# Gate's early load behind a piece of w_in, a fourth place in the rings of the output columns, and a seventh pair of seven products

## The chip, the cores and the metric

The kernel runs on one core of one Trainium2 chip. The metric is the device time of one execution in microseconds (us), lower is better. The kernel before has a median of 918.88 us in three runs (916.53 to 919.73).

Engines are called by their names in the profile: PE multiplies matrices (PEld loads its stationary operand), DVE and ACT work elementwise, POOL too, SP issues most of the DMA transfers. Each engine, and SP's queue of transfers too, works strictly in the order in which its instructions stand; an instruction that has to wait holds up all behind it.

## The reference

One layer of a decoder on 256 tokens (T), width D = 2048, inner width E = 4096, all in float32:

```python
h = rmsnorm(x, norm_g)                                  # (1, 256, 2048)
mod = einsum('bd,df->bf', silu(c), ada_w) + ada_b       # ada_w: 2048 x 6144
shift, scale, gate = split(mod, 3)
h = h * (1 + scale) + shift
proj = einsum('bsd,de->bse', h, w_in)                   # w_in: 2048 x 16384
b_gate, c_gate, v, g = split(proj, 4)
u = causal_depthwise_conv(c_gate * v, conv_w)           # width 3
y = b_gate * u * silu(g)                                # (1, 256, 4096)
out = rmsnorm(x + gate * einsum('bse,ed->bsd', y, w_out), final_g)   # w_out: 4096 x 2048
```

Of the 218 MB of weights most is w_in (134 MB); every weight is read once or, with the sums below, a little more.

## The kernel before

**High and low parts.** PE works on a rounded float32 here. Each float32 operand is split into a high part (a cast on ACT, L380) and a low part (what is left, a subtraction on DVE, L385), and each product is the sum of three: high by high, high by low, low by high. So a piece of weights that comes in as `raw` needs a place for its high part `hi` and one for its low part `lo`. The transposed activations `hT` hold both parts already: k 0 to 13 (blocks of 128 of D) in one tile `big`, k 14 and 15 in `big2`.

**Rings.** A place holds 2048 float32 columns on 128 partitions (1 MB). `w_tile(kind, ...)` hands out places in rings of three: "raw", "hi" and "lo". In the second phase "raw" takes the pieces of w_in and "lo" their low parts. In the output phase it is the other way round: the pieces of w_out and the sums made of them lie in the ring "lo", their low parts in the ring "raw"; only pair 0 of the first columns is loaded into the ring "raw".

**First phase** (up to 377 us): the first half of w_in, and the sums of silu(c) with ada_w for shift and scale. Nothing of it changes.

**Second phase** (loop at L798): the channel tiles 16 to 31 in twos, four quarters of w_in each (b_gate, c_gate, v, g), two pieces of eight k each: 64 pieces of 1 MB, loaded by SP (L804). A piece costs PE 48 matmuls of 128x256 into the bank `mm_b` (L545). At the end of a quarter DVE and ACT take the bank away (L827, L828, L830). Behind each piece stand two calls:

- `gate_piece()`: one of 32 pieces of the gate's sums over ada_w (loads `at_g`, sums on DVE in `gacc`, L711). When a quarter of the gate is complete, POOL folds its 128 partitions in seven steps, a DMA and an addition each (L715 to L717), and adds the row to `gate_row` in DRAM.
- `early_weights()`: a table `EARLY`, by the count of pieces, says what else is done. For a pair of `SEVEN_2` it loads a block of w_out (`raw_u`, L755), makes its sums on DVE (L769, L772, L773) and stores them to DRAM from ACT's queue (`made`, L780). "gate" loads a quarter of `gate_row` into `turned` (L786), which is the tile z0 and so in the trace `z<-gate_row`; POOL's folds use the same tile `turned`. "gated" multiplies a block of w_out with it.

**Output** (`columns`, L943): y by w_out. A pair is 256 of the 4096 channels. The first call makes the output's first 1024 columns from all 16 pairs (`mm_w`, matmuls 128x512, L888), the second the next 512 columns and, for the pairs it has, the last 512 (`mm_o`). A plain pair costs 24 matmuls. A pair in `SEVEN` or `SEVEN_2` costs 21: instead of the eight products of 2 x 2 blocks by 2 x 2 blocks it makes seven (`seven`, L904), from sums of the weights' blocks (`sums_o`, made by DVE at L769 to L773, or loaded from `made`) and from sums of the tokens (`form`). In the banks `mm_1` and `mm_7` the products stand that `gather` adds afterwards. Then come pairs 4 to 7 for the third 512 columns, the gated blocks for the last 512, and the residual, norm and stores.

In the first columns pieces and sums go round in six places (`wide_ring`): the three of the ring "lo" and three in the tile `big`, in which hT lay. From n = 13 (`AT_END`) on, `big` takes half of x, final_g and u2. In the second columns they go round in four (`next_ring`) until twelve are given out, then in three.

**What sets the order.** The code's order is only a start: a scheduler puts each engine's instructions in order by when it expects places and operands to come free. Starts that are pinned by `add_manual_dep` come behind the instruction they name.

Of the kernel before, what the change touches and what calls it, by code (L numbers as in the profile page):

```python
# [13 lines left out]
P = 128  # L14
# [103 lines left out]
def short_conv_layer(ctx: ExitStack, tc: tile.TileContext, x, c, norm_g, ada_w, ada_b, w_in, conv_w, w_out, final_g, out):  # L118
# [21 lines left out]
    nth = {"raw": 0, "hi": 0, "lo": 0}  # L140

# [157 lines left out]
    junk = hpool.tile([P, TT, HX], F32, tag="big", name="junk")  # L299
# [18 lines left out]
    KB = KT - 2  # L318
    hT = hpool.tile([P, KB, 2 * T], F32R, tag="big", name="hT")
    hT2 = hpool.tile([P, KT - KB, 2 * T], F32R, tag="big2", name="hT2")  # L320

    def tokens(k, part):
        return (hT[:, k] if k < KB else hT2[:, k - KB])[:, part * T : (part + 1) * T]
# [352 lines left out]
    def gate_columns(c0, n):  # L676
        flat = gate_slots[c0 // 1024].rearrange("p h s f -> p (h s f)").bitcast(F32)
        return flat[:, c0 % 1024 : c0 % 1024 + n]
# [3 lines left out]

    def load_gate(j):

        c0 = j * 1024
        nc.sync.dma_start(gate_columns(c0, 1024), gate_row[0:1, c0 : c0 + 1024].partition_broadcast(P))
# [38 lines left out]
    SEVEN_2 = range(10, 16)  # L725
# [39 lines left out]
    passed = [0]  # L765

# [8 lines left out]
    def early_weights():  # L775

        while to_store:
            unit, sums = to_store.pop()
            made[unit] = dram.tile([P, SLOT], F32, tag=f"made{len(made)}", name="made")
            nc.scalar.dma_start(made[unit], sums)  # L780
        unit = EARLY.get(passed[0])
        passed[0] += 1
        if unit is None:
            return
        if unit == "gate":
            nc.sync.dma_start(turned, gate_row[0:1, 3 * W : 4 * W].partition_broadcast(P))  # L786
            return
        raw, sums = raw_tile("raw_u"), w_tile("lo", "sums_u")
        blocks, out = (v.rearrange("p (b f) -> p b f", f=W) for v in (raw, sums))
        if not isinstance(unit, int):  # L790
            load_o(raw, unit[1] * EP, EP, 3 * W, W)
            nc.vector.tensor_tensor(out=out, in0=blocks, in1=turned.unsqueeze(1).to_broadcast([P, EP, W]), op=ALU.mult)
        else:
            load_o(raw, 2 * unit, 2, 2 * W, 2 * W)
            list(sums_of(blocks, out))
        to_store.append((unit, sums))

    for ct in range(NS, NCT, 2):  # L798
        for q in QUARTERS:
            bank = psum.tile([P, CT, T], F32, tag="mm", name="mm_b")[:, 0:2]  # L800
            col = q * E + ct * P
            for kp in range(0, KT, KP):
                raw = raw_tile("raw")
                nc.sync.dma_start(  # L804
# [34 lines left out]
    big = hpool.tile([P, 3 * D + W], F32, tag="big", name="big")  # L839
    xh = big[:, 0 : TT * D].rearrange("p (h t f) -> p h t f", h=2, t=TT)  # L840
    HD = D // 2

    def xr(t, c0, n):
        return xh[:, c0 // HD, t, c0 % HD : c0 % HD + n]

    def load_x(h):
        for t in range(TT):
            nc.sync.dma_start(xh[:, h, t], x[t * P : (t + 1) * P, h * HD : (h + 1) * HD])

    fg = big[:, TT * D : 3 * D]  # L850
    u2 = big[:, 3 * D :]
    ends = [z.rearrange("p a b f -> p (a b f)").rearrange("p (h f) -> p h f", h=2) for z in zs]

    places6 = [None] * 3 + [big[:, i * SLOT : (i + 1) * SLOT] for i in range(3)]
    taken, ending = [0], [False]

    def wide_ring(name):

        i = taken[0] % 6 if not ending[0] else 0
        taken[0] += 1  # L860
        return w_tile("lo", name) if places6[i] is None else places6[i]
# [12 lines left out]
    last_silu = ended_silu[0]  # L874
# [22 lines left out]
    def weighted(t, c0, n, pr, at):  # L897
# [4 lines left out]
        nc.vector.tensor_tensor(out=r, in0=r, in1=fg[:, c0 : c0 + n], op=ALU.mult)  # L902
# [40 lines left out]
    def columns(c0, order, sevens, bank, p1, p6, p75, whole, loads=None, ring=None):  # L943


        for n, j in enumerate(order):
            raw = w_tile("raw", "raw_o") if n == 0 and c0 == 0 else ring("raw_o")
# [10 lines left out]
            if j in sevens:  # L958
                sums = ring("sums_o")
# [20 lines left out]
    def wide_bank(name):  # L980
# [6 lines left out]
        lambda t, d: wide[t][:, d], *extra_banks(), p75, True, load_ends, wide_ring,  # L987
# [10 lines left out]
    def finish(t):  # L998
# [4 lines left out]
        for c0, n, vector in ((0, 512, True), (512, 512, False), (1536, 512, True), (1024, 512, False)):  # L1003
            dd = slice(c0, c0 + n)
            r = xr(t, c0, n)
            if c0 == 1536:
                nc.vector.scalar_tensor_tensor(out=r, in0=po[t], scalar=fs, in1=fg[:, dd], op0=ALU.mult, op1=ALU.mult)
# [5 lines left out]

    AT_X = 8
    taken[0] = 0

    def next_ring(name):

        i = taken[0] % 4
        taken[0] += 1  # L1020
        return big[:, SLOT : 2 * SLOT] if i == 3 and taken[0] <= 12 else w_tile("lo", name)

# [4 lines left out]
        2 * W, (0, 1, 10, 2, 11, 3, 12, 13, 8, 14, 15, 9), SEVEN_2,  # L1027
        lambda t, d: halves[d][:, t], *po, p75, False, lambda n: load_x(1) if n == AT_X else None, next_ring,
# [81 lines left out]
```

## Time and profile before

| | us |
|---|---|
| median of 3 runs | 918.88 |
| the profiled execution, its time | 917.02 |
| its span | 915.2 |
| PE busy | 888.6 |
| DVE busy | 695.4 |
| ACT busy | 490.5 |
| POOL busy | 88.0 |

The profile is of one execution. The span is what lies between its first and last instruction; 1.8 us of the execution's time lie around it. The mean granted clock of PE is 0.991. In the rows that are shown below, a timeline has the start, the duration, the engine with its line, the operation, what it writes and reads, the shape and the count, and in brackets the idle time before it with what ended that. A row of the windows has the stretch and its length, then busy time and count of PE, PEld, DVE, ACT and POOL, PE's granted clock, the DMA engines' busy share and GB/s. A row of the DMA issues has the count, KB each and the median time from issue to landing. A row of the waits has the sum, the count and the longest.

### The profile page before, as it was taken

The page shows a single profiled execution, that of the slowest core. Times are in us where ns is not written, and L with a number is a line of the kernel's source. Part 1 is how long each engine was busy: PE and PEld are TensorE (multiplying, and loading weights), DVE is VectorE, ACT ScalarE, POOL GpSimd, SP SyncE. Part 2 cuts the span into 40 slices and gives each one's busy share as a digit, 9 for nine tenths or more (in the row PEclk, how much of TensorE's full clock was granted, in tenths as well). Part 3 has the DMA queues.
Part 4 walks back from the last instruction along what each step waited for, and adds up shares of the span by engine and source line. Part 5 has one row for each costly group of instructions (what it writes and reads, how often), then busy time and mean ns, then how long its engine had stood idle before and what let it go on. Part 6 is the DMA issues. An engine that isn't in the chain of part 4 may idle for free.

```text
span 915.2 us, 16520 instructions
## 1 busy us (share of the span) xinstructions
PE 888.6 (97%) x6977; PEld 849.9 (93%) x6977; DVE 695.4 (76%) x693; ACT 490.5 (54%) x436; POOL 88.0 (10%) x108
## 2 busy tenths in 40 slices
PE   7999999999999999999999999949999999999996
PEld 4999999999999999999999999949999988778885
DVE  5889998889987876858865786537667668999775
ACT  6768866565558765644344434234434454545553
POOL 0000000010000234410132012400000000000000
PEclk9999999999999999999999999979999999999999
DMA  9999999999997688777877889489889877686872
GB/s 307 368 370 365 365 321 354 341 363 351 380 344 258 189 279 238 237 215 222 271 230 219 273 270 307 142 286 301 290 286 289 306 264 244 197 294 235 302 280 92
DMA packets 164873, 257.29 MB, mean 281 GB/s; under 512 B 7668, under 2 KB 106580, under 8 KB 162624
## 3 DMA queue, kind: packets, MB, share of 16 engines
q1 hardware_dynamic: 159680, 239.89, 79.5%
q0 software_dynamic: 3840, 7.94, 3.2%
q10 hardware_dynamic: 1280, 8.43, 2.3%
q8 instruction: 54, 0.88, 0.4%
q14 instruction: 19, 0.16, 0.0%
HBM read 237.86 MB, written 10.50 MB: 271 GB/s over the span
## 4 chain that ended last, share of the span: by engine, by line
PE 79%; DMA 11%; DVE 4%; ACT 2%; POOL 2%; issue 1%; SPq 0%; ACTq 0%; POOLq 0%; DVEq 0%
PE mm_s L545 38%; PE mm_b L545 27%; PE mm_o L888 6%; PE mm L888 4%; DMA z<-gacc 3%; PE mm_w L888 3%; DMA at_g<-in_ada_w_dram 3%; DVE lo L385 2%; DMA at<-in_ada_w_dram 2%; ACT hi L380 2%; POOL gacc L717 1%; DMA raw_o<-in_sc_w_out_dram 1%; DMA raw<-in_sc_w_in_dram 1%; POOL z L715 0%; DVE gacc L711 0%
## 5 line engine op out<-in xcount | busy, mean ns | idle before, releaser
L545 PE MATMUL mm_b<-hT,hi 128*128 128x256 f32 x2048 | 349.9, 277 | 11.4 <-ACT hi L380 11.4
L545 PE MATMUL mm_s<-hT,hi 128*128 128x256 f32 x2048 | 336.3, 277 | 0.0
L545 PEld LDWEIGHTS mm_b<-hT,hi 128*128 128x128 f32 x2048 | 309.3, 188 | 11.6 <-ACT hi L380 11.6
L545 PEld LDWEIGHTS mm_s<-hT,hi 128*128 128x128 f32 x2048 | 299.7, 188 | 0.2
L545 PE MATMUL mm_b<-hT,lo 128*128 128x256 f32 x1024 | 283.4, 277 | 1.5 <-DVE lo L385 1.5
L545 PE MATMUL mm_s<-hT,lo 128*128 128x256 f32 x1024 | 261.7, 277 | 0.0
L380 ACT CAST hi<-raw 128x2048 fp32r<-128x2048 f32 (+1 forms) x66 | 123.8, 1876 | 206.9 <-PE mm_b L545 94.0
L385 DVE TENSOR_TENSOR lo<-raw,hi 128x2048 fp32r<-128x2048 f32 (+1 forms) x66 | 153.3, 2328 | 78.6 <-ACT hi L380 63.1
L545 PEld LDWEIGHTS mm_b<-hT,lo 128*128 128x128 f32 x1024 | 192.9, 188 | 1.8 <-DVE lo L385 1.8
L545 PEld LDWEIGHTS mm_s<-hT,lo 128*128 128x128 f32 x1024 | 182.7, 188 | 0.0
L385 DVE TENSOR_TENSOR lo<-raw_s,hi 128x2048 fp32r<-128x2048 f32 (+1 forms) x80 | 149.0, 1868 | 29.9 <-ACT hi L380 29.3
L380 ACT CAST hi<-raw_s 128x2048 fp32r<-128x2048 f32 (+2 forms) x81 | 124.0, 1541 | 70.2 <-PE mm_s L545 42.9
L515 DVE SCALAR_TENSOR_TENSOR gv<-at,silu_c,gv 128x512 f32<-128x512 f32 x105 | 78.8, 751 | 10.3 <-DMA at<-in_ada_w_dram 8.6
L568 ACT COPY acc<-mm_s 128x1024 f32<-128x1024 f32 x54 | 54.6, 1011 | 26.9 <-PE mm_s L545 26.8
L717 POOL TENSOR_TENSOR gacc<-gacc,z 128x512 f32<-128x512 f32 x28 | 44.2, 1577 | 103.4 <-DMA z<-gacc 103.4
L888 PE MATMUL mm_w<-hi,y 128*128 128x512 f32 x160 | 51.4, 390 | 0.3 <-ACT hi L380 0.3
L711 DVE SCALAR_TENSOR_TENSOR gacc<-at_g,silu_c,gacc 128x512 f32<-128x512 f32 x60 | 45.0, 749 | 7.4 <-DMA at_g<-in_ada_w_dram 6.3
L888 PE MATMUL mm_o<-hi,y 128*128 128x512 f32 x152 | 48.3, 389 | 0.0
L582 ACT COPY mm_s<-acc 128x1024 f32<-128x1024 f32 x38 | 38.6, 1015 | 2.6 <-DVE acc L571 1.8
L380 ACT CAST hi<-raw_o 128x2048 fp32r<-128x2048 f32 x14 | 26.7, 1909 | 22.1 <-DMA raw_o<-in_sc_w_out_dram 16.8
L385 DVE TENSOR_TENSOR lo<-raw_o,hi 128x2048 fp32r<-128x2048 f32 x14 | 32.1, 2289 | 6.8 <-ACT hi L380 6.7
L888 PEld LDWEIGHTS mm_w<-hi,y 128*128 128x128 f32 x160 | 30.0, 188 | 6.9 <-ACT hi L380 0.7
(191 smaller groups left out, 745.6 us busy)
## 6 DMA issues: line engine op xcount, KB each, us to landing
raw<-in_sc_w_in_dram SPq DMA_DIRECT2D x64, 1024.0 KB, 6.2
raw_s<-in_sc_w_in_dram SPq DMA_DIRECT2D x47, 1024.0 KB, 8.2
at<-in_ada_w_dram SPq DMA_DIRECT2D x126, 256.0 KB, 7.9
raw_o<-in_sc_w_out_dram SPq DMA_DIRECT2D x17, 1024.0 KB, 6.0
raw_s<-in_sc_w_in_dram SPq DMA_DIRECT2D x33, 512.0 KB, 7.2
at_g<-in_ada_w_dram SPq DMA_DIRECT2D x32, 512.0 KB, 8.2
raw_u<-in_sc_w_out_dram SPq DMA_DIRECT2D x8, 1024.0 KB, 5.7
made<-sums_u ACTq DMA_DIRECT2D x8, 1024.0 KB, 6.9
```

The lines of the kernel that those rows point to most:

```text
L380: nc.scalar.copy(hi[:, :n], raw[:, :n])
L385: last_low[0] = nc.vector.tensor_tensor(out=lo[:, :n], in0=raw[:, :n], in1=hi[:, :n].bitcast(F32), op=ALU.subtract)
L515: nc.vector.scalar_tensor_tensor(out=gv, in0=at4[:, i], scalar=c_k, in1=gv, op0=ALU.mult, op1=ALU.add)
L545: mm = last_mm[0] = nc.tensor.matmul(dst, w, h[k], start=begins and left, stop=ends, skip_group_check=True)
L568: nc.scalar.copy(acc[ch, q], bank)
L582: nc.scalar.copy(bank, acc[ch, q])
L711: nc.vector.scalar_tensor_tensor(out=ga, in0=at3[:, i, :], scalar=s, in1=ga, op0=ALU.mult, op1=ALU.add)
L717: nc.gpsimd.tensor_tensor(out=ga, in0=ga, in1=turned, op=ALU.add)
L888: nc.tensor.matmul(dst, y[a], b, start=opens and i == 0, stop=ends and i == 2, skip_group_check=True)
```

## The change

1. hT lies in five tiles: `b0`, `b1`, `b2` (k 0 to 3, 4 to 7, 8 to 11; a place each), `b3` (k 12, 13) and `big2` (k 14, 15). So a part of it comes free when the last matmul on these k is done.
2. From the start of the output, `fourth` gives each of the rings "lo", "hi" and "raw" a fourth place: b0, b1, b2. This holds for the first columns until n = 10. From n = 13 on b0 takes half of x, b2 (`closing`) half of final_g and half of the gate, and b1 is the fourth place of "lo", until n = 5 of the second columns. `places6`, `wide_ring` and `next_ring` are gone.
3. `SEVEN_2` has a seventh pair, 9, and the second columns another order. Its early units stand at every third count from 33 instead of every fourth from 35, and the other three units at 56, 58, 61 instead of 58, 59, 62.
4. The early load of the gate is tied behind the load of the piece of w_in that was issued last in the code.

```diff
     def w_tile(kind, name, dtype=F32, i=None):
         if i is None:
-            i = nth[kind] % 3
-            nth[kind] += 1
+            size = 4 if kind in fourth else 3
+            i = nth[kind] % size
+            nth[kind] = i + 1
+        if i == 3:
+            return hpool.tile([P, SLOT + 64], dtype, tag=fourth[kind], name=name)[:, 16 : 16 + SLOT]
         return wpool.tile([P, SLOT], dtype, tag=f"{kind}{i}", name=name, bufs=1)
...
-    KB = KT - 2
-    hT = hpool.tile([P, KB, 2 * T], F32R, tag="big", name="hT")
-    hT2 = hpool.tile([P, KT - KB, 2 * T], F32R, tag="big2", name="hT2")
+    hT = [hpool.tile([P, SLOT + 64], F32R, tag=f"b{g}", name="hT") for g in range(3)]
+    hT += [hpool.tile([P, 4 * T], F32R, tag=tag, name="hT") for tag in ("b3", "big2")]
...
-    SEVEN_2 = range(10, 16)
+    SEVEN_2 = range(9, 16)
...
-    EARLY = {35 + 4 * i: j for i, j in enumerate(SEVEN_2)}
-    EARLY.update({58: "gate", 59: ("gated", LAST[0]), 62: ("gated", LAST[1])})
+    EARLY = {33 + 3 * i: j for i, j in enumerate(SEVEN_2)}
+    EARLY.update({56: "gate", 58: ("gated", LAST[0]), 61: ("gated", LAST[1])})
...
         if unit == "gate":
-            nc.sync.dma_start(turned, gate_row[0:1, 3 * W : 4 * W].partition_broadcast(P))
+            load = nc.sync.dma_start(turned, gate_row[0:1, 3 * W : 4 * W].partition_broadcast(P))
+            tc.add_manual_dep(load.ins, last_load[0].ins.name, after, reason="the gate is done by then")
             return
...
-                nc.sync.dma_start(
+                last_load[0] = nc.sync.dma_start(
...
     def load_ends(n):
-        ending[0] = n >= AT_END
-        if n == AT_END - 2:
-            load_gate(0)
+        if n == AT_END - 3:
+            fourth.clear()
         elif n == AT_END:
             load_x(0)
-        elif n == AT_END + 1:
-            nc.sync.dma_start(fg, final_g.rearrange("(o d) -> o d", o=1).partition_broadcast(P))
-            load_gate(1)
+            closing.append(hpool.tile([P, D], F32, tag="b2", name="closing"))
+            load_fg(0)
+            load_broadcast(HD, gate_row[0:1, 0:HD])
+            fourth["lo"] = "b1"
+    fourth.update({"lo": "b0", "hi": "b1", "raw": "b2"})
...
-            raw = w_tile("raw", "raw_o") if n == 0 and c0 == 0 else ring("raw_o")
+            raw = w_tile("raw" if n == 0 and c0 == 0 else "lo", "raw_o")
...
+    def load_last(n):
+        if n == AT_X - 3:
+            fourth.clear()
+        elif n == AT_X:
+            load_x(1)
+            nc.sync.dma_start(gate_columns(HD, HD), gate_row[0:1, HD:D].partition_broadcast(P))
+            load_fg(1)
...
-        2 * W, (0, 1, 10, 2, 11, 3, 12, 13, 8, 14, 15, 9), SEVEN_2,
+        2 * W, (0, 9, 1, 10, 11, 2, 12, 13, 3, 14, 15, 8), SEVEN_2,
```

SP's queue in the second phase, before, around the gate load (`z0`): raw are pieces of w_in, raw_u the blocks of the early units.

```order
L755 DMA raw_u_6749<-in_sc_w_out_dram 128x2x1024 [waits DMAHW7_49,DMAHW4_49,DVE_49]
L804 DMA raw_6763<-in_sc_w_in_dram 128x8x256 [waits DMAHW5_49,DVE_49]
L804 DMA raw_6819<-in_sc_w_in_dram 128x8x256 [waits DMAHW6_49,DMAHW1_49,DVE_49]
L804 DMA raw_6876<-in_sc_w_in_dram 128x8x256 [waits DMAHW7_49,DVE_49]
L804 DMA raw_6930<-in_sc_w_in_dram 128x8x256 [waits DMAHW0_49,DVE_49]
L755 DMA raw_u_6984<-in_sc_w_out_dram 128x2x1024 [waits DMAHW1_49,DVE_49]
L786 DMA z0_4482<-gate_row_4486 128x512 [waits DMASW4_49,DMASW3_49,DMASW5_49,DMASW2_49,DMASW6_49,DMASW1_49,DMASW7_49,DMASW0_49,Pool_49]
L804 DMA raw_7001<-in_sc_w_in_dram 128x8x256 [waits DMAHW3_49,DVE_49]
L804 DMA raw_7057<-in_sc_w_in_dram 128x8x256 [waits DMAHW4_49,DVE_49]
```

The same queue after, around the same load, now L789; the first raw_u shown is that of the seventh pair, and the line numbers of the others are L757 for L755 and L808 for L804.

```order
L757 DMA raw_u_7712<-in_sc_w_out_dram 128x2x1024 [waits DMAHW7_49,DVE_49]
L808 DMA raw_7726<-in_sc_w_in_dram 128x8x256 [waits DMAHW0_49,DMAHW4_49,DVE_49,Activation_49]
L808 DMA raw_7782<-in_sc_w_in_dram 128x8x256 [waits DMAHW2_49,DVE_49]
L808 DMA raw_7839<-in_sc_w_in_dram 128x8x256 [waits DMAHW3_49,DVE_49]
L808 DMA raw_7893<-in_sc_w_in_dram 128x8x256 [waits DMAHW4_49,DVE_49]
L808 DMA raw_7959<-in_sc_w_in_dram 128x8x256 [waits DMAHW5_49,DMAHW1_49,DVE_49]
L789 DMA z0_4485<-gate_row_4489 128x512 [waits DMASW4_49,DMASW3_49,DMASW5_49,DMASW2_49,DMASW6_49,DMASW1_49,DMASW7_49,DMASW0_49,Pool_49]
L808 DMA raw_8014<-in_sc_w_in_dram 128x8x256 [waits DMAHW7_49,DVE_49]
```

The load has moved from behind the second raw_u to behind all seven and the loads of five more pieces. Its list of waits is the same.

SP's queue where the output begins, before: raw_o_8426 is pair 0, raw_o_8486 pair 8 and raw_o_8456 pair 1, and `big` are pairs 2 and 9.

```order
L804 DMA raw_8350<-in_sc_w_in_dram 128x8x256 [waits DMAHW6_49,DVE_49]
L755 DMA raw_o_8426<-in_sc_w_out_dram 128x2x1024 [waits DMAHW0_49,DVE_49]
L755 DMA raw_o_8486<-in_sc_w_out_dram 128x2x1024 [waits DMAHW4_49,DVE_49]
L755 DMA raw_o_8456<-in_sc_w_out_dram 128x2x1024 [waits DMAHW7_49,PE_49]
L755 DMA big_8416<-in_sc_w_out_dram 128x2x1024 [waits PE_49]
L755 DMA big_8416<-in_sc_w_out_dram 128x2x1024
```

After, raw_o_8467 is pair 1, raw_o_8497 pair 8, raw_o_8437 pair 0, raw_o_8562 pair 9 and raw_o_8532 pair 2:

```order
L808 DMA raw_8363<-in_sc_w_in_dram 128x8x256 [waits DMAHW1_49,DVE_49]
L757 DMA raw_o_8467<-in_sc_w_out_dram 128x2x1024 [waits DMAHW5_49,DVE_49,PE_49]
L757 DMA raw_o_8497<-in_sc_w_out_dram 128x2x1024 [waits DVE_49,PE_49]
L757 DMA raw_o_8437<-in_sc_w_out_dram 128x2x1024 [waits DMAHW0_49,PE_49]
L757 DMA raw_o_8562<-in_sc_w_out_dram 128x2x1024 [waits DMAHW6_49,DVE_49]
L757 DMA raw_o_8532<-in_sc_w_out_dram 128x2x1024 [waits DMAHW2_49,PE_49]
```

Pair 0 has moved from the first to the third place and now waits for PE: it lies in b2, where hT's k 8 to 11 are. Pair 8 waits for PE's matmuls on b0.

PE's queue where the output begins, before (hi_8428 and lo_8430 are the parts of pair 0):

```order
L545 MATMUL mm_b_8291<-hT2_174,lo_8354 128x256
L888 MATMUL mm_w_8422<-hi_8428,y0_3413 128x512 [waits Activation_49]
L888 MATMUL mm_w_8422<-lo_8430,y0_3413 128x512 [waits DVE_49]
L888 MATMUL mm_w_8422<-hi_8428,y0_3413 128x512 x2
L888 MATMUL mm_w_8422<-lo_8430,y0_3413 128x512
```

And after (hi_8500, lo_8501 are pair 8's parts, hi_8507 the high part of its sums, hi_8439 and lo_8441 the parts of pair 0):

```order
L550 MATMUL mm_b_8306<-hT_177,lo_8367 128x256
L891 MATMUL mm_1_8435<-hi_8500,y8_4475 128x512 [waits Activation_49]
L891 MATMUL mm_1_8435<-lo_8501,y8_4475 128x512 [waits DVE_49]
L891 MATMUL mm_1_8435<-hi_8500,y8_4475 128x512
L891 MATMUL mm_1_8436<-hi_8507,gate0_4483 128x512 [waits Activation_49]
L891 MATMUL mm_w_8433<-hi_8439,y0_3416 128x512 [waits PE_49,Activation_49]
L891 MATMUL mm_w_8434<-hi_8439,y0_3416 128x512 [waits PE_49]
L891 MATMUL mm_7_8432<-hi_8507,gate0_4483 128x512 [waits PE_49]
L891 MATMUL mm_w_8433<-lo_8441,y0_3416 128x512 [waits DVE_49]
```

Three matmuls of pair 8 and one of its sums now stand ahead of the first of pair 0, and the one that reads pair 0's low part is the eighth.

More of the change, by code (lines that the diff above doesn't have):

```diff
@@ L941, in gather, with columns @@
         add(ends[1][:, 0], p75[:, 1], ends[1][:, 1])
-    def columns(c0, order, sevens, bank, p1, p6, p75, whole, loads=None, ring=None):
+    def columns(c0, order, sevens, bank, p1, p6, p75, whole, loads=None):
         for n, j in enumerate(order):
-            raw = w_tile("raw", "raw_o") if n == 0 and c0 == 0 else ring("raw_o")
+            raw = w_tile("raw" if n == 0 and c0 == 0 else "lo", "raw_o")
             ready = c0 > 0 and j in made
@@ L958, in columns @@
             if j in sevens:
-                sums = ring("sums_o")
+                sums = w_tile("lo", "sums_o")
                 if ready:
```

50 lines of the change are left out of this document (23 added, 27 removed).

## The prediction

> **What bounds the kernel now.** I read the page first: busy times, slices, and the chain that ended last.
>
> ```profile
> PE 888.6 (97%) x6977; PEld 849.9 (93%) x6977; DVE 695.4 (76%) x693; ACT 490.5 (54%) x436; POOL 88.0 (10%) x108
> ...
> PE   7999999999999999999999999949999999999996
> ...
> PEclk9999999999999999999999999979999999999999
> ...
> DMA  9999999999997688777877889489889877686872
> ```
>
> PE is the bound: 97% of the span. One slice out of 40, at 594 to 618 us, has both PE and its clock low, and DMA in it is at 4 tenths. So next the table of waits, of PE from 560 us on, and the row of SP's queue that falls in that slice.
>
> ```profile
> PE mm_b L545 <- ACT hi L380: 11.4, 1, 11.4
> PE mm_b L545 <- DVE lo L385: 1.5, 1, 1.5
> PE mm L888 <- DVE lo L918: 1.0, 2, 0.6
> PE mm_w L888 <- ACT hi L380: 0.3, 1, 0.3
> SPq L786 <- DMA z<-gacc: 15.9, 1, 15.9
> ```
>
> After 560 us PE waits 14.2 us in all, 12.9 of them once, in the second phase. What the cast waited for is in the timelines of SP and PE:
>
> ```profile
> 575.93 0.37 SPq L755 DMA_DIRECT2D raw_u<-in_sc_w_out_dram  x1
> 596.25 0.34 SPq L786 DMA_DIRECT2D z<-gate_row  x1
> 596.70 12.07 SPq L804 DMA_DIRECT2D raw<-in_sc_w_in_dram  x4
> 594.39 0.28 PE L545 MATMUL mm_b<-hT,lo 128*128 128x256 f32 x1
> 606.10 0.80 PE L545 MATMUL mm_b<-hT,hi 128*128 128x256 f32 x2 [11.43 <-ACT hi L380]
> 608.42 0.58 PE L545 MATMUL mm_b<-hT,lo 128*128 128x256 f32 x1 [1.53 <-DVE lo L385]
> ```
>
> Between 575.93 and 596.25 SP issues nothing. It stands at the gate load (L786), which waits until POOL's folds have written `gate_row`; the w_in loads queue behind it. PE runs dry at 594.67 and gets its next piece at 606.10: 596.70 plus load plus cast. This wait is what the change goes at.
>
> **Part 1, the gate load behind a piece.** In SP's new order the load stands some 24 issues later, behind the loads of piece 56. The folds still end near 596 us; piece 56 comes 80 us later, so the wait has nothing left to wait for, and POOL's folds have the same place in their own queue. What goes is 11.43 + 1.53 = 12.96 us of idle time, and slow matmuls behind it:
>
> ```profile
> 598.00:599.00 1.00, 0.00 (x0) 0.00 (x0) 0.00 (x0) 0.00 (x0) 0.00 (x0) 0.50 0.77 199
> 612.00:613.00 1.00, 1.00 (x11) 1.00 (x10) 0.00 (x0) 0.63 (x1) 0.00 (x0) 1.00 0.93 271
> 609.45 0.63 PE L545 MATMUL mm_b<-hT,hi 128*128 128x256 f32 x2
> 610.09 0.63 PE L545 MATMUL mm_b<-hT,hi 128*128 128x256 f32 x2
> 613.07 0.39 PE L545 MATMUL mm_b<-hT,hi 128*128 128x256 f32 x2
> 613.41 0.39 PE L545 MATMUL mm_b<-hT,hi 128*128 128x256 f32 x2
> ```
>
> From one such row to the next stand three matmuls. They take 0.64 us at granted clock 0.50 and 0.34 at 1.00: 0.213 against 0.113 each. Half clock lasts from 608.42 to about 611.2 (the 0.41 us matmuls end there), so 2.8 x (1 - 0.113/0.213) = 1.3 us, and 0.2 for the two matmuls at 606.10. **Sum -14.5 us.** What hides a late w_in load then is the lead of three buffers; part 5 asks whether it is enough.
>
> The Trainium skill ("TensorE: Matmul & The Clock Gate", Part 1) says the clock halves after an idle window of about 3.4 us and needs about 3.4 busy us to come back. The trace has 2.8 us back; by the page's figure the part above would be about 14.8 and not 14.5.
>
> **Part 2, the first output columns open late.** This is the term that decides. Now the last matmul of the second phase passes to the first of the output without a gap:
>
> ```profile
> 723.86 11.49 SPq L755 DMA_DIRECT2D raw_o<-in_sc_w_out_dram  x3
> 740.12 0.28 PE L545 MATMUL mm_b<-hT,lo 128*128 128x256 f32 x1
> 740.23 0.39 PE L888 MATMUL mm_w<-hi,y 128*128 128x512 f32 x1
> 740.43 0.69 DVE L830 TENSOR_TENSOR z<-mm_b,z 128x512 f32<-128x512 f32 x1 [5.00 <-PE mm_b L545]
> 742.07 1.90 ACT L380 CAST hi<-raw_o 128x2048 fp32r<-128x2048 f32 x1 [7.55 <-DMA raw_o<-in_sc_w_out_dram]
> 743.87 1.47 ACT L914 CAST hi<-raw_o 128x1536 fp32r<-128x1536 f32 x1
> 744.00 2.29 DVE L385 TENSOR_TENSOR lo<-raw_o,hi 128x2048 fp32r<-128x2048 f32 x1 [2.35 <-ACT hi L380]
> 746.21 1.22 DVE L769 TENSOR_TENSOR sums_o<-raw_o 128x1024 f32<-128x1024 f32 x1
> raw_o<-in_sc_w_out_dram SPq DMA_DIRECT2D x17, 1024.0 KB, 6.0
> ```
>
> Pair 0's weights were issued at 723.86, 16.5 us ahead of the end E = 740.4 of the mm_b matmuls. Pair 0 takes the ring of w_in pieces, which after the change has a fourth place: k 8 to 11 of hT. That place is free only when the last piece is nearly through, 12 matmuls or 1.4 us before E. SP's new order therefore has pair 1 first, then pair 8 (whose place, hT k 0 to 3, comes free one piece of 48 x 0.113 = 5.4 us before E), then pair 0. PE's new order opens with pair 8 and needs pair 0's two parts in its first ten rows.
>
> I follow the queues with the landing of 6.0 us. Pair 8 is there at E + 0.6. DVE: first sums (1.22) to 1.8, L830 (0.69) to 2.5, a second sums step and two short ones beside it to 3.8, the third to 4.4 (steps of about 0.6, read off L830's pace for 512 columns). ACT casts the sums only then (1.90) to 6.3, and pair 0 behind them (1.90) to 8.2, though pair 0 landed at E + 4.6. DVE makes pair 0's low part (2.29): E + 10.5. PE has done 7 matmuls of 128x512 in between (1.6 us) and starts again at half clock (1.4, as in part 1): 10.5 - 1.6 + 1.4 = **+10.3 us**. With a landing a microsecond shorter it is 9.3, longer 11.3. From below: if nothing but pair 0's own load, cast and subtraction counted, 4.6 + 1.90 + 2.29 = 8.8, and with the same two corrections 8.6; a landing shorter by 1 us gives 7.6. Nothing covers it: PE has no other work there.
>
> **Part 3, a seventh seven-product pair** in the second columns replaces 24 matmuls by 21.
>
> ```profile
> 880.24 16.81 PE mm_o L888 x74
> 820.00:840.00 20.00, 20.00 (x90) 16.57 (x89) 19.83 (x15) 11.82 (x9) 0.00 (x0) 1.00 0.74 251
> sums_o<-made SPq DMA_DIRECT2D x3, 1024.0 KB, 7.1
> raw_o<-in_sc_w_out_dram SPq DMA_DIRECT2D x4, 512.0 KB, 5.5
> raw_o<-in_sc_w_out_dram SPq DMA_DIRECT2D x2, 1024.0 KB, 6.7
> ```
>
> 16.81 / 74 = 0.227 us; three of them are **-0.7**. Its two extra transfers (sums stored and loaded) lie beside other work.
>
> **Part 4, buffers in the output.** First columns: a fourth place for high and low parts can only shorten the 1.0 + 0.3 us of waits there, but pieces and sums share four places where they had six: **-0.6**, between 0 and -1.3. At the opening of the second columns the seven-pair 9 now comes second and pair 1 third, in a stretch where DVE is busy 19.83 of 20 us and PE just does not wait. A seven-pair puts its own low part (some 1.7 us) ahead of pair 1's and takes 0.7 us less of PE: pair 1 is up to 2.4 us later than PE wants. Some slack must be there, unseen: I take half, **+1.2**, bounds 0 and 2.4. From the sixth pair on these columns now have three places for pieces and sums where before a fourth lasted almost to the end. What is left is 3 plain pairs and 4 sevens, 156 matmuls, 35.4 us, and 11 fillings, so three places must turn round in 9.65 us. One turn is landing + 1.90 + 2.29 + about 0.2, so a landing over 5.25 us costs 11/3 of the excess. The three rows give a mean of (4 x 7.1 + 4 x 5.5 + 3 x 6.7)/11 = 6.4, less 0.36 since the sevens' pieces need shorter casts: 2.9 us, less a lead that I cannot see. Bounds 0 and 2.9; I take **+1.2**.
>
> **Part 5, denser sums.** From count 33 a unit follows every three pieces, not four.
>
> ```profile
> 634.00:656.00 22.00, 22.00 (x196) 22.00 (x196) 14.93 (x14) 8.63 (x8) 0.00 (x0) 1.00 0.89 294
> 551.00:576.00 25.00, 25.00 (x223) 25.00 (x222) 15.27 (x15) 10.51 (x8) 6.59 (x7) 1.00 0.99 307
> ```
>
> A period of four pieces (21.8 us) moves 6 MB, 289 GB/s; the first row shows 294 at a share of 0.89. Three pieces (16.3 us) move 5 MB = 5.24e6 bytes: 320 GB/s, by that row a share of 0.97. By the second, 307 at 0.99, the period would take 17.1 us and each of six would lose 0.7. I stay near the first, whose mix of transfers is the same: **+0.5**, between 0 and 4.3.
>
> The Trainium skill ("DMA: Bandwidth & Descriptors", Where 436 GB/s comes from) puts a core's share of HBM at about 358 GB/s. By that page 320 fits and this part is 0; the row at 307 with the engines full speaks for the dearer side.
>
> **Sum:** -14.5 + 10.3 - 0.7 - 0.6 + 1.2 + 1.2 + 0.5 = -2.6. The profiled execution took 917.02 (span 915.2), 1.9 less than the median 918.88 of three. From the one that gives 914.4, from the other 916.3; I predict the middle, 915.3, and 911.5 to 919 for this case alone.
>
> **The rivals.**
> - *The opening is cheap.* For it: ACT may be less in the way than its queue says, and parts 4 and 5 may cost nothing. With 7.6 for part 2 and zero for the costs, -14.5 + 7.6 - 0.7 - 1.3 = -8.9: 908 to 910. Against: the order in each queue is fixed, and pair 0, issued at E - 1.4, is not there before E + 3.6 even with a landing of 5 us.
> - *The whole gain.* If I misread which place pair 0 waits for, nothing stands against the 15 us: 901 to 904. The order of issues speaks against it.
> - *Slower: three places in the second columns.* If landings there are like the longest row, 7.1, and a bit over (7.35), the cost is 3.67 x 2.1 = 7.7 us, not 1.2: +3.9, 921 to 923. Without the lead it passes the gain of 2.6 at a landing of about 6.3 after the 0.36 is taken off, against 6.05 by the rows. For it: DMA will be denser than now; against: the table of waits has none in mm_o, with such landings today.
> - *DMA-bound units.* 4.3 in place of 0.5: +1.2, 918 to 920.
> - *The change doesn't do what it says:* the gate load still holds SP up, at its new place. Part 1 falls, the rest stays: 929. It would need folds that end 80 us later than now.
>
> **How the numbers follow.** A measurement of this kernel tells 0.3%, 2.8 us, from no change: faster is below 916.1, slower above 921.6. Chances: forecast 0.62 (of it faster 0.36, same 0.25, slower 0.01); cheap opening 0.13, faster; whole gain 0.05, faster; three places 0.11 (same 0.04, slower 0.07); DMA-bound 0.08 (same 0.06, slower 0.02); no effect 0.01, slower. Faster 0.54, same 0.35, slower 0.11. The range 907 to 921 leaves out the whole gain and the end of the slower cases, some 0.14.
>
> **What would show it.** Right: no wait of SP at the gate load and none of PE near 594; a gap of PE of 8 to 10 us, broken by seven matmuls, where mm_b ends, its releasers the cast and subtraction of raw_o, with clock 0.5 behind; pair 0's issue about 1.4 us before the end of mm_b; waits of a microsecond or two in mm_o. Wrong: mm_b passing to the output without a gap (then 901 to 904), waits of mm_b for hi L380 recurring at every third piece, or SP waiting in the second columns for buffers by more than 3 us in all that PE pays for.

## The result, and the profile after

The changed kernel takes 930.46 us (median of 6 runs, 926.84 to 932.46), the kernel before 916.45 in the same comparison (915.44 to 919.73): ratio 1.0139, interval 1.0110 to 1.0167. It is **slower by 14 us**; forecast were 915.3 and a range up to 921. The profiled execution took 930.47, span 928.7 against 915.2.

First the page of after, busy times and slices, as shown of before:

```profile
PE 894.3 (96%) x6974; PEld 850.9 (92%) x6974; DVE 701.4 (76%) x697; ACT 491.9 (53%) x437; POOL 94.9 (10%) x108
...
PE   7999999999999999999999999989999899999896
...
PEclk9999999999999999999999999999999989999999
...
DMA  9999999999997687867787988997998646688762
```

The one deep notch of before is gone; several shallow ones are there instead. PE's waits from 560 us on (sum, count, longest):

```profile
PE mm_b L550 <- DVE lo L390: 10.2, 10, 2.6
PE mm L891 <- DVE lo L921: 3.1, 1, 3.1
PE mm L891 <- ACT hi L920: 2.8, 1, 2.8
PE mm L891 <- DVE lo L390: 1.4, 1, 1.4
PE mm L891 <- ACT hi L917: 1.2, 1, 1.2
```

No wait on ACT at the gate load, but ten on DVE in the second phase. Where the time went by stage is read from the view of one tile: count, shortest, median and longest duration in ns, then the first and last start. mm_b of before and after, then mm_o of before and after:

```profile
L545 PE MATMUL mm_b<-hT,hi x2048: 276/276/579, 376.9 to 740.0; 128*128 128x256 f32 x187
L888 PE MATMUL mm_o<-hi,y x152: 388/389/395, 824.7 to 896.7; 128*128 128x512 f32 x152
```

```profile
L550 PE MATMUL mm_b<-hT,hi x2048: 276/276/284, 376.1 to 737.9; 128*128 128x256 f32 x187
L891 PE MATMUL mm_o<-hi,y x140: 387/389/628, 831.3 to 910.0; 128*128 128x512 f32 x140
```

From such rows this table is made for all kernels (from mm_b's first to its last start; from there to mm_o's first; mm_o's first to last), in us. A stage is that of the one profiled execution; the time is the median of all runs, beside the median of before on the same chip:

| kernel | mm_b | first columns | mm_o | time | before |
|---|---|---|---|---|---|
| before | 363.1 | 84.7 | 72.0 | | 916.45 |
| after | 361.8 | 93.4 | 78.7 | 930.46 | 916.45 |
| e1_dep | 348.0 | 84.7 | 72.7 | 901.29 | 916.78 |
| e2_units4 | 358.8 | 100.2 | 76.7 | 930.47 | 916.78 |
| e3_pair0 | 359.5 | 83.5 | 78.8 | 919.50 | 916.78 |
| e4_ring | 360.4 | 93.9 | 75.1 | 925.71 | 916.78 |
| e8_phase | 348.0 | 95.5 | 76.9 | 917.97 | 916.00 |
| e9_all | 351.1 | 89.8 | 73.7 | 910.28 | 916.00 |
| e11_33 | 355.2 | 84.9 | 72.2 | 910.10 | 916.00 |
| e14_tied | 348.0 | 85.6 | 72.3 | 902.15 | 917.32 |
| e15_tied3 | 356.3 | 93.2 | 75.3 | 923.94 | 917.32 |
| e16_half | 348.3 | 93.2 | 75.6 | 915.27 | 916.26 |
| e5_bytes | 347.9 | 85.2 | 72.0 | 912.01 | 916.00 |
| e5b_bytes | 353.6 | 87.2 | 72.3 | 907.31 | 917.32 |
| e12_best | 349.3 | 84.5 | 76.1 | 906.43 | 917.32 |
| e17_six | 347.9 | 90.0 | 72.6 | 906.73 | 916.26 |

After against before: -1.3, +8.7 and +6.7, and -0.8 ahead of mm_b and +0.2 behind mm_o: 13.5, the difference of the spans. The tied gate load had taken 15 us out of mm_b (e1_dep below), so almost all of that was lost again there: 10.2 us in the ten waits of the list, and some 0.36 us more around each of them than the list counts.

The opening of the output, in after's timelines of PE, ACT and DVE, each row a start and a duration:

```profile
738.01 0.28 PE L550 MATMUL mm_b<-hT,lo 128*128 128x256 f32 x1
739.53 0.50 PE L891 MATMUL mm<-hi,y 128*128 128x512 f32 x1 [1.24 <-ACT hi L917]
743.18 0.80 PE L891 MATMUL mm<-lo,y 128*128 128x512 f32 x1 [3.15 <-DVE lo L921]
745.32 1.22 PE L891 MATMUL mm_w<-hi,y 128*128 128x512 f32 x2 [0.49 <-ACT hi L385]
747.64 0.80 PE L891 MATMUL mm_w<-lo,y 128*128 128x512 f32 x1 [0.68 <-DVE lo L390]
741.56 1.90 ACT L385 CAST hi<-sums_o 128x2048 fp32r<-128x2048 f32 x1 [1.07 <-DVE sums_o L776]
743.37 1.89 ACT L385 CAST hi<-raw_o 128x2048 fp32r<-128x2048 f32 x1
745.29 2.29 DVE L390 TENSOR_TENSOR lo<-raw_o,hi 128x2048 fp32r<-128x2048 f32 x1 [1.04 <-ACT hi L385]
```

This is part 2 as it was written: pair 0's cast behind the cast of pair 8's sums, its low part ready 9.3 us after the end of mm_b at 738.3, seven matmuls in between. From 742 to 750 us the granted clock is 0.50.

### The profile page after: what moved, and what is told of

It reads as the page before. It is cut to its first block, busy times and chain, and to the rows that moved or that the text cites. A ratio compares the mean times of both kernels' runs of the same rounds, so it can differ in the third digit from the quotient of the medians.

```text
span 928.7 us, 16537 instructions
## 1 busy us (share of the span) xinstructions
PE 894.3 (96%) x6974; PEld 850.9 (92%) x6974; DVE 701.4 (76%) x697; ACT 491.9 (53%) x437; POOL 94.9 (10%) x108
## 3 DMA queue, kind: packets, MB, share of 16 engines
q1 hardware_dynamic: 160256, 241.72, 78.7%
## 4 chain that ended last, share of the span: by engine, by line
PE 67%; DMA 16%; DVE 10%; ACT 4%; issue 3%; SPq 0%; ACTq 0%; DVEq 0%
PE mm_s L550 33%; PE mm_b L550 22%; DMA raw<-in_sc_w_in_dram 6%; DVE lo L390 5%; PE mm_w L891 5%; PE mm_o L891 4%; ACT hi L385 3%; PE mm L891 3%; DMA at<-in_ada_w_dram 3%; DMA at_g<-in_ada_w_dram 3%; DMA raw_o<-in_sc_w_out_dram 1%; DMA raw_s<-in_sc_w_in_dram 1%; DMA raw_u<-in_sc_w_out_dram 1%; DMA sums_o<-made 1%; DVE sums_u L772 0%
## 5 line engine op out<-in xcount | busy, mean ns | idle before, releaser
L550 PE MATMUL mm_b<-hT,hi 128*128 128x256 f32 x2048 | 349.3, 276 | 0.0
L550 PE MATMUL mm_b<-hT,lo 128*128 128x256 f32 x1024 | 284.3, 278 | 10.2 <-DVE lo L390 10.2
L520 DVE SCALAR_TENSOR_TENSOR gv<-at,silu_c,gv 128x512 f32<-128x512 f32 x105 | 78.8, 751 | 10.6 <-DMA at<-in_ada_w_dram 8.9
L719 POOL TENSOR_TENSOR gacc<-gacc,z 128x512 f32<-128x512 f32 x28 | 49.8, 1780 | 116.5 <-DMA z<-gacc 116.5
L891 PE MATMUL mm_w<-hi,y 128*128 128x512 f32 x160 | 53.8, 402 | 0.5 <-ACT hi L385 0.5
L390 DVE TENSOR_TENSOR lo<-raw_o,hi 128x2048 fp32r<-128x2048 f32 x17 | 38.8, 2289 | 17.9 <-ACT hi L385 17.9
L385 ACT CAST hi<-raw_o 128x2048 fp32r<-128x2048 f32 x17 | 32.4, 1908 | 30.7 <-PE mm_w L891 11.7
L390 DVE TENSOR_TENSOR lo<-sums_o,hi 128x2048 fp32r<-128x2048 f32 x15 | 34.4, 2291 | 11.6 <-ACT hi L385 11.5
```

The lines of the kernel that those rows point to most:

```text
L385: nc.scalar.copy(hi[:, :n], raw[:, :n])
L390: last_low[0] = nc.vector.tensor_tensor(out=lo[:, :n], in0=raw[:, :n], in1=hi[:, :n].bitcast(F32), op=ALU.subtract)
L520: nc.vector.scalar_tensor_tensor(out=gv, in0=at4[:, i], scalar=c_k, in1=gv, op0=ALU.mult, op1=ALU.add)
L550: mm = last_mm[0] = nc.tensor.matmul(dst, w, h[k], start=begins and left, stop=ends, skip_group_check=True)
L719: nc.gpsimd.tensor_tensor(out=ga, in0=ga, in1=turned, op=ALU.add)
L891: nc.tensor.matmul(dst, y[a], b, start=opens and i == 0, stop=ends and i == 2, skip_group_check=True)
```

## Experiments: the gate load, the opening, the second columns

**e1_dep.** The kernel before with the tie alone.

```diff
-            nc.sync.dma_start(turned, gate_row[0:1, 3 * W : 4 * W].partition_broadcast(P))
+            load = nc.sync.dma_start(turned, gate_row[0:1, 3 * W : 4 * W].partition_broadcast(P))
+            tc.add_manual_dep(load.ins, last_load[0].ins.name, after, reason="the gate is done by then")
...
-                nc.sync.dma_start(
+                last_load[0] = nc.sync.dma_start(
```

> The kernel before, with nothing but the gate's early load tied behind the load of a piece of w_in. Theory (the wait at the gate load costs what part 1 of the prediction says, and nothing else is late behind it): the mm_b stretch goes from 363.5 us to about 349, the rest stays, time 902 (-14.5 on 916.5). Rival (the lead of three buffers is used up elsewhere, so the w_in pieces are late a little further on): a gain under 8 us, with new waits of mm_b on ACT hi or DVE lo.

Measured 901.29, ratio 0.9834 (0.9819 to 0.9848). mm_b fell by 15.1 to 348.0, and no other stage moved by more than 0.7:

```profile
L545 PE MATMUL mm_b<-hT,hi x2048: 276/276/276, 375.6 to 723.6; 128*128 128x256 f32 x187
```

This one tie is the best version that was found; it beats both kernels.

**e3_pair0.** After, with the fourth places from the second pair on.

```diff
-        if n == AT_END - 3:
+        if n == 1:
+            fourth.update({"lo": "b0", "hi": "b1", "raw": "b2"})
+        elif n == AT_END - 3:
...
-    fourth.update({"lo": "b0", "hi": "b1", "raw": "b2"})
```

> The changed kernel, with the fourth places given out only from the second pair on, so that pair 0 is loaded into an ordinary place as before. Theory (the late opening is pair 0's place under hT): SP issues pair 0 some 15 us before the end of mm_b, mm_w begins without a gap, the stretch from the end of mm_b to the first mm_o falls from 93 to 83 to 85 us, time 920 to 922. Rival (the opening waits for pair 8 and its sums too, which stay under hT): the gap only moves behind pair 0's matmuls, a gain of 4 us at most.

The first columns went from 93.4 to 83.5. In its timeline mm_b and mm_w meet without a gap:

```profile
735.21 0.28 PE L550 MATMUL mm_b<-hT,lo 128*128 128x256 f32 x1
735.33 0.39 PE L892 MATMUL mm_w<-hi,y 128*128 128x512 f32 x1
```

So giving out the fourth places one pair too early costs 9.9 us; the rival falls, since pair 0's own matmuls cover pair 8's sums.

**e4_ring.** After, with the second columns' fourth place kept.

```diff
-        if n == AT_X - 3:
+        if n == AT_X:
             fourth.clear()
-        elif n == AT_X:
```

> The changed kernel, with the fourth place for pieces and sums kept in the second columns until n = 8 and not n = 5. Theory (the waits in mm_o, 4.9 us and the half clock behind the longest, are three places that turn too slowly): the 2.8 us wait goes, the mm_o stretch falls by 4 to 6 us, time 925. Rival (they come from the order, pair 9 in second place, and from DVE): no change, or under 1.5 us.

Time -4.8, mm_o 75.1. But e2, e3, e8 and e15 have after's rings in the second columns, and their mm_o takes 75.3 to 78.8; the last has after's order of loads there too. So the size of this effect is not settled: a gain of the ring, or a good execution.

**e12_best.** e1_dep with the seventh pair alone: units at 31 + 4i, the second columns in the order (0, 1, 9, 10, 2, 11, 12, 3, 13, 14, 15, 8). Its pair 9 reads the gate where its token sums were, so those products are not the layer's.

> e1_dep with the seventh seven-product pair alone: units at 31, 35, ... 55, pair 9 third in the second columns, all rings as before. If the seventh pair is worth its three matmuls of 128x512 (0.7 us) and nothing is late behind it: 900 to 901 against 901.3 for e1_dep. If its two extra loads are late in the second columns: 902 to 905, with waits in mm_o.

906.43: mm_o takes 76.1 where six pairs took 72.7. The pair that saves three matmuls costs, with its place in the order, 3.4 us and not -0.7. Its loads are late: PE's longest wait in mm_o, 1.4 us, stands behind a cast that waited 3.2 us for `sums_o<-made`. Each such pair loads 256 + 512 + 1024 KB in the time of 21 matmuls, a plain one 1024 KB in that of 24.

## Experiments: the units

**e2_units4.** After, units at every fourth count again.

```diff
-    EARLY = {33 + 3 * i: j for i, j in enumerate(SEVEN_2)}
-    EARLY.update({56: "gate", 58: ("gated", LAST[0]), 61: ("gated", LAST[1])})
+    EARLY = {33 + 4 * i: j for i, j in enumerate(SEVEN_2)}
+    EARLY.update({58: "gate", 59: ("gated", LAST[0]), 62: ("gated", LAST[1])})
```

> The changed kernel with its seven units at every fourth count again (33, 37, ... 57; gate 58, gated 59 and 62). Theory (the ten waits of mm_b on DVE lo, 10.2 us, come from the units at every third piece): they go, the mm_b stretch falls from 362 to 349 to 351 us, time 917 to 920 against 930.5. Rival (they come from POOL's folds, which now end 20 us later and lie beside the first units): the waits before 620 us stay, a gain of 3 us at most.

No gain. The theory fell, and of the rival only the figure held: mm_b took 358.8, with waits on DVE lo up to 2.9 us also behind 620 us, where POOL's folds are over. The 3.0 us that mm_b gained the opening lost again: the first columns took 100.2, and PE waited there 6.5 us for one cast. Six units in the same spacing from 35 had 348.0 in mm_b (e1_dep), so the count of the first unit came under suspicion.

**e8_phase** has `31 + 4 * i` in that table, **e11_33** is e1_dep with `33 + 4 * i` in place of `35 + 4 * i`.

> The changed kernel with its seven units at 31, 35, ... 55 (gate 58, gated 59 and 62). Theory (where a unit falls): the mm_b stretch is 348 to 351 us where e2_units4, with the units at 33, 37, ... 57, had 359; the opening of the output stays late (93 to 100 us for the first columns), time 917 to 921. Rival (seven units are one too many at any place, or the first one falls into POOL's folds): mm_b stretch 355 or more.

> e1_dep (the kernel before with the tied gate load, 901.3) with one number changed: its six units start at count 33 and not 35, still every fourth. Bytes, places and number of units are the same. New theory (the waits of mm_b come from where a unit falls among the quarters: at 33 its three sums stand on DVE between the closing steps of a quarter, which wait for ACT behind a cast that waits for a load, so the block's place comes free late): mm_b waits on DVE lo return, the mm_b stretch is 354 to 359 us and not 348, time 907 to 912. Rival (the waits come from the number of bytes or units): no change, 901 to 902.

Both as the new theory had it: 348.0 with seven units at 31, 35, ... (the rest of the kernel being after's); 355.2 and 910.10 with six at 33, 37, .... The mechanism stands in e11_33's timelines of DVE, ACT, PE and SP's queue:

```profile
647.12 0.69 DVE L481 TENSOR_TENSOR y<-z,y 128x512 fp32r<-128x512 f32 x1 [2.54 <-ACT y L480]
647.73 0.69 DVE L774 TENSOR_TENSOR sums_u<-raw_u,sums_u 128x512 f32<-128x512 f32 x1
648.45 0.37 SPq L806 DMA_DIRECT2D raw<-in_sc_w_in_dram  x1
657.27 1.92 ACT L380 CAST hi<-raw 128x2048 fp32r<-128x2048 f32 x1 [5.94 <-DMA raw<-in_sc_w_in_dram]
659.22 2.29 DVE L385 TENSOR_TENSOR lo<-raw,hi 128x2048 fp32r<-128x2048 f32 x1 [5.56 <-ACT hi L380]
661.54 0.37 SPq L806 DMA_DIRECT2D raw<-in_sc_w_in_dram  x1
666.94 0.69 DVE L773 TENSOR_TENSOR sums_u<-raw_u,sums_u 128x512 f32<-128x512 f32 x1
668.39 1.91 ACT L380 CAST hi<-raw 128x2048 fp32r<-128x2048 f32 x1 [5.54 <-DMA raw<-in_sc_w_in_dram]
670.20 0.90 ACT L471 ACTIVATE z<-z,cw 128x256 f32<-128x256 f32 x2
670.74 0.88 DVE L472 SCALAR_TENSOR_TENSOR z<-z,cw,z 128x255 f32<-128x255 f32 x2 [3.11 <-ACT z L471]
671.54 0.68 DVE L774 TENSOR_TENSOR sums_u<-raw_u,sums_u 128x512 f32<-128x512 f32 x1
672.25 0.37 SPq L806 DMA_DIRECT2D raw<-in_sc_w_in_dram  x1
675.27 0.58 PE L545 MATMUL mm_b<-hT,lo 128*128 128x256 f32 x1 [2.35 <-DVE lo L385]
```

The rows hold two units, and one place can be followed through the first six. The first unit's third sum (L774 at 647.73) stands behind the low part of y (L481), which waits 2.5 us for ACT. Only when it is done is the block's place free, and SP issues the next piece of w_in into it at 648.45. That piece is cast at 657.27, after ACT has waited 5.9 us for it; its low part ends at 661.51, and the place's next load goes out at 661.54. This piece is late in turn (cast at 668.39), and PE waits 2.35 us for its low part. The second unit has the same fault: its third sum, at 671.54, stands behind a step of the convolution (L472), which waits for ACT's L471 behind that late cast, 3.9 us after the second sum is done, and the place's next load goes out only at 672.25.

**e14_tied.** e11_33, with these steps tied behind the unit's last sum:

```diff
-            list(sums_of(blocks, out))
+            last = list(sums_of(blocks, out))[-1]
+            for op in closers:
+                tc.add_manual_dep(op.ins, last.ins.name, after, reason="the sums come first")
...
```

`closers` are the DVE instructions of the convolution and of y's low part of the quarter closed last. Against e11_33, SP, ACT, PE and POOL have the same order, and on DVE five groups of instructions stand one place further down.

> e11_33 (units at 33, 37, ...; 910.1, mm_b stretch 355.4) with nothing moved but DVE's order: the steps of a quarter's closing that wait for ACT (the convolution and the low part of y) are tied behind the third sum of the unit that stands beside them. Theory (a third sum that stands behind such a step keeps the block's place, and the next piece of w_in is late): the mm_b stretch falls back to 348 to 350 us, time 901 to 903. Rival (units at these counts cost what they cost by when their loads fall, whatever DVE's order): 354 to 356 us, 908 to 911.

902.15, mm_b 348.0: the theory held, and the rival falls. DVE's timeline of the second of the two units now has the three sums together, and no wait between them:

```profile
659.53 1.22 DVE L775 TENSOR_TENSOR sums_u<-raw_u 128x1024 f32<-128x1024 f32 x1
660.78 0.69 DVE L778 TENSOR_TENSOR sums_u<-raw_u,sums_u 128x512 f32<-128x512 f32 x1
661.51 0.69 DVE L779 TENSOR_TENSOR sums_u<-raw_u,sums_u 128x512 f32<-128x512 f32 x1
662.12 0.87 DVE L477 SCALAR_TENSOR_TENSOR z<-z,cw,z 128x255 f32<-128x255 f32 x2
```

**e15_tied3** and **e16_half.** After with the same tie (only DVE's order changes, at two places), and that with only half of each unit's sums stored; the second columns then load this half twice, so their products are not the layer's:

```diff
-            nc.scalar.dma_start(made[unit], sums)
+            if isinstance(unit, int):
+                nc.scalar.dma_start(made[unit][:, 0 : SLOT // 2], sums[:, 0 : SLOT // 2])
+            else:
+                nc.scalar.dma_start(made[unit], sums)
...
-                    nc.sync.dma_start(sums, made[j])
+                    for h in range(2):
+                        nc.sync.dma_start(sums[:, h * 1024 : h * 1024 + 1024], made[j][:, 0:1024])
```

> The changed kernel (units at every third piece, mm_b stretch 361.9) with the same tie as in e14_tied. Theory (DVE's order alone): 348 to 352 us in mm_b, time 917 to 920 against 930.5. Rival (four fills of three places in three pieces, with landings of 9 to 12 us, are too many whatever DVE's order): 356 us or more, 924 or more.

> e15_tied3 (units at every third piece, DVE's order tied; mm_b stretch 356.3) with only the first half of each unit's sums stored: 4.5 MB in place of 5 in a period of three pieces, 289 GB/s, what the kernel before asks. In the second columns the first half is loaded twice in place of both halves. The places and their fills are the same. If bytes make up what is left of the waits: mm_b stretch 348 to 351 us, time 916 to 919. If four fills of three places do: 354 to 357 us, 922 to 925.

mm_b of the two, in this order:

```profile
L555 PE MATMUL mm_b<-hT,hi x2048: 276/276/286, 376.7 to 733.0; 128*128 128x256 f32 x187
L555 PE MATMUL mm_b<-hT,hi x2048: 276/276/286, 376.3 to 724.6; 128*128 128x256 f32 x187
```

The tie takes 5.5 us off mm_b, taking half a megabyte off each period another 8.0: 361.8, 356.3, 348.3. So the rival of e15_tied3 had the figure (356 or more) and not the reason. (e3_pair0 and e4_ring, with after's order in this stage, have 359.5 and 360.4, so the 5.5 is known to some 2 us; the medians differ by 6.5.) The places and their fills were the same in the last step, and so was DVE's order but for one step, so it is bytes. One other way is open in principle: a shorter store also gives the sums' own place back sooner. But in none of the three kernels does the list of waits have DVE's low parts waiting for that store between 545 and 725 us. The windows from 560 to 677 of after, e15_tied3 and e16_half, in this order (length, busy time and count of PE, PEld, DVE, ACT, POOL, clock, DMA share, GB/s):

```profile
560.00:677.00 117.00, 106.82 (x915) 104.69 (x914) 76.24 (x66) 42.66 (x33) 17.10 (x17) 1.00 0.92 300
```

```profile
560.00:677.00 117.00, 111.40 (x964) 109.83 (x964) 72.22 (x67) 44.12 (x35) 11.51 (x14) 1.00 0.91 307
```

```profile
560.00:677.00 117.00, 116.98 (x1032) 116.79 (x1031) 81.75 (x73) 49.24 (x39) 12.51 (x14) 1.00 0.93 297
```

No kernel here moves more than 308 GB/s over these 117 us, with waits (e3_pair0, e5b_bytes) or without (e8_phase); what asks for 320 in its periods waits, though the DMA engines' share is 0.91 or 0.92 and not 1. It is no fixed ceiling: over 20 us e5b_bytes moves up to 332, from 680 to 700. The landings tell it too; DMA issues of 545 to 677 us, after first, then e1_dep:

```profile
raw<-in_sc_w_in_dram SPq DMA_DIRECT2D x23, 1024.0 KB, 9.3
raw_u<-in_sc_w_out_dram SPq DMA_DIRECT2D x7, 1024.0 KB, 10.7
```

```profile
raw<-in_sc_w_in_dram SPq DMA_DIRECT2D x24, 1024.0 KB, 7.6
raw_u<-in_sc_w_out_dram SPq DMA_DIRECT2D x6, 1024.0 KB, 6.8
```

**e5_bytes** and **e5b_bytes** come at the same from the other side: e1_dep and an extra store of 0.7 MB behind each unit (the edit of e5b_bytes; e5_bytes has it without `stored` and the tie).

```diff
-            nc.scalar.dma_start(made[unit], sums)
+            stored = nc.scalar.dma_start(made[unit], sums)
+            if isinstance(unit, int):
+                spare = dram.tile([P, 1360], F32, tag=f"spare{unit}", name="spare")
+                more = nc.scalar.dma_start(spare, hT[:, 0:3].rearrange("p k f -> p (k f)")[:, 0:1360].bitcast(F32))
+                tc.add_manual_dep(more.ins, stored.ins.name, after, reason="beside the sums")
```

> e1_dep with an extra store of 0.7 MB from hT to DRAM behind each of its six units: 7.0 MB in 21.8 us, the 320 GB/s that the changed kernel asks of the DMA engines, with the units where they were. Theory (where a unit falls): mm_b stretch 348 to 350 us, time 901 to 903. Rival (320 GB/s is more than the transfers can give): a period of four pieces takes 7.0 MB at about 305 GB/s = 24 us, so 1.5 to 2.2 us of waits for each of six units, mm_b stretch 355 to 361 us, time 908 to 914.

> e5_bytes mended: its extra stores had no operand that held them back and all went out in the first phase. Now each is tied behind the store of its unit's sums, so that a period of four pieces moves 7.0 MB in 21.8 us, 320 GB/s. Theory (bytes are not the cause): mm_b stretch 348 to 350 us, time 901 to 903. Rival (320 GB/s is too much): 355 to 361 us, 908 to 914.

In e5_bytes the scheduler put all six stores into the first phase, where mm_s (the first phase's matmuls) then waited 7.3 us once: 912.01, which says nothing of the question. e5b_bytes takes 907.31 and has mm_b at 353.6: 5.6 us for bytes, with the units at good counts and DVE's order that of e1_dep but for one step. (Its profile is of the slowest of its four runs; the medians differ by 6.0 in all.) The theory that bytes do not matter falls; the rival's 355 to 361 was too dear.

## Experiments: the repairs together

> The changed kernel with three repairs: units as in e8_phase, fourth places only from the second pair on (e3_pair0), the fourth place of the second columns kept until n = 8 (e4_ring). Theory (the three costs are apart from each other): 348 to 351 + 83 to 84 + 75, against 361.9 + 93.3 + 78.7 in the changed kernel, so 903 to 905. Rival (the parts interact: the fourth places bring something that shows only when the others are gone): 908 or more.

> e9_all with six pairs of seven products in the second columns and in the order of the kernel before, units at 35, 39, ... 55. If the second columns of the changed kernel lose by the seventh pair and its place in the order: mm_o stretch 72 to 73 us, mm_b 348, and with the fourth places from the second pair on 83.5 us for the first columns, so 899 to 901. If they lose by their rings or by the loads of x and final_g beside them: mm_o stretch 74 or more, 903 or more.

e17_six has, on top of e9_all, `SEVEN_2 = range(10, 16)`, units from 35 and the second columns' old order. e9_all: 910.28, as its rival had it; e17_six: 906.73. mm_o is back at 72.6 with six pairs, so the new rings with the longer fourth place cost the second columns nothing. With seven pairs and the new order e9_all has 73.7, only 1.1 more, where e12_best paid 3.4. How the 6.7 us that after lost there split between the seventh pair, its order, the fourth place that ends early and the spread between executions is therefore not settled. But the first columns take 89.8 and 90.0 where e3_pair0 had 83.5. In e9_all SP's queue has the loads of x, final_g and the gate ahead of a pair's weights that they followed in e3_pair0 (x alone stood ahead there), and PE waits 0.8 and 2.1 us behind them:

```profile
767.84 0.81 SPq L852 DMA_DIRECT2D xr<-in_x_dram  x2
770.60 0.33 SPq L858 DMA_DIRECT2D closing<-in_final_g_dram  x1
770.97 0.43 SPq L858 DMA_DIRECT2D closing<-gate_row  x1
771.45 17.87 SPq L757 DMA_DIRECT2D raw_o<-in_sc_w_out_dram  x4
788.98 0.74 PE L892 MATMUL mm<-lo,y 128*128 128x512 f32 x1 [2.14 <-DVE lo L922]
```

In e17_six the waits of the first columns are others (1.6 us at the opening, 1.4 and 1.6 later). That the loads' order is the cause was not tried by itself. Either way the repairs do not add up: of 348 + 83.5 + 72.6, which e8_phase, e3_pair0 and e17_six have one by one, e17_six has 347.9 + 90.0 + 72.6. e9_all's mm_b, 351.1 where e8_phase with the same counts had 348.0, is not explained either.

## Why the prediction was wrong

Of the forecast -2.6 us, -14.0 were to come in mm_b, +9.7 in the first columns and +1.7 in mm_o. The profiles show -1.3, +8.7 and +6.7: 12.7 us too much in mm_b, 5.0 in mm_o.

- **Part 1 was right.** -14.5 forecast; e1_dep shows 15.1 in the stage and 15.5 in the time. Its rival, that the load still holds SP up, fell. Two readings beside it were off and cost nothing: the DMA slice at 4 tenths is the one before PE's notch (572 to 595 us, when SP issued nothing), and the folds, said to end near 596 still, end near 617 in after, 60 us before the gate load.
- **Part 2 was right**, in mechanism and size: 10.3, or 9.3 with a landing of 5 us, was forecast, and pair 8 was there at the end of mm_b, as with 5 us (its cast began at 738.0). With the 0.6 of part 4 the first columns were to lose 9.7; they lost 8.7, and e3_pair0 gives back 9.9.
- **Part 5 is the step that failed.** "I stay near the first, whose mix of transfers is the same: **+0.5**, between 0 and 4.3." It cost 13.8 us: 361.8 against 348.0 in e1_dep, and in e8_phase, which differs from after in the units' counts alone. Two things were wrong in it. The first is the row: the one at 294 GB/s and a share of 0.89 was read as 11% in hand, and e5b_bytes shows that 320 was not to be had without waits. The second row was nearer, but its 4.3 would have been too little as well: bytes made 8.0 us (e15_tied3 to e16_half), of which 5.6 are listed waits and the rest time around them. The second is that the sums were weighed only as bytes, not as DVE instructions in an order: two of after's units have their last sum behind a step that waits for ACT, worth 5.5 us (e15_tied3). The order of DVE could be read beforehand, as SP's and PE's were for the opening.
- **Part 3 and the second columns.** Forecast -0.7 for the seventh pair, +1.2 and +1.2 for order and ring; mm_o took 6.7 more. The -0.7 was wrong: the pair's loads were called hidden, and with its order it cost 3.4 in e12_best and 1.1 from e17_six to e9_all. The ring's part is open within the 3.5 us by which mm_o differs between kernels that have the same rings there.
- **The rivals.** DMA-bound units and three places were named, at 4.3 and 7.7 in place of 0.5 and 1.2, each alone. Both stages lost time together: from the middle 915.3, +3.8 and +6.5 give 925.6, nearer to what was measured than either. With chances of 0.08 and 0.11 and no case for both, the range ended at 921. The part that DVE's order played was in none of them.

The Trainium skill's figure of about 358 GB/s for a core ("DMA: Bandwidth & Descriptors", Where 436 GB/s comes from), by which 320 would fit, is a limit that this mix of loads and stores stayed well below: 308 GB/s was the most over the 117 us, and taking the demand to 289 ended the waits. The first phase, nearly all loads, had 344 GB/s over its first 300 us in the kernel before; why the mix gives less was not tried.

## What to carry to other kernels

Where an order is fixed, read what stands ahead of an instruction that frees a buffer: a step that waits for another engine there holds the buffer, and by it the load. The rate to count with is the highest that the trace shows over a long stretch of the same mix, not the room that a busy share seems to leave. And try the parts of a change one by one: here one tie gives 15 us, and the rest takes 29.

## What was not expected of the hardware

With the units closer together, the median landing of a unit's block went from 6.8 us (e1_dep) to 10.7 (after), at nearly the same rate (300 GB/s in the window of after above, 298 in that of e1_dep): the loads took longer to land and brought hardly more bytes. And two neighbouring stages vary unequally: mm_b takes 347.9 to 348.3 in every kernel in which PE's list has no wait there, while mm_o, where loads are just in time, takes 75.3 to 78.8 with one and the same set of rings.
